# A third FFN with seven quarter products, and the modulation steps given out anew

## The chip, the cores and the metric

One Trainium2 chip, one core of it. The metric is device microseconds of one launch. The kernel before was timed three times: 2214.08, 2215.94 and 2216.86 us, median 2215.94 us.

## The reference, cut to what matters

Two layers over x of 512 tokens by 1024 features, all in float32. Each layer is FFN, mixer, FFN (the mixer is MLA attention in layer 0 and RWKV-7 in layer 1), and each of the six branches is modulated by vectors that come from one conditioning vector c:

```python
c_act = silu(c)
for i in range(2):
    mods = (c_act @ ada_w[i] + ada_b[i]).reshape(B, 3, 3, 1024)     # shift, scale, gate of three branches
    h = rmsnorm(x, g[i,0]) * (1 + mods[:,0,1]) + mods[:,0,0]
    x = x + 0.5 * mods[:,0,2] * swiglu(h, ffn_w_in[i,0], ffn_w_out[i,0])
    h = rmsnorm(x, g[i,1]) * (1 + mods[:,1,1]) + mods[:,1,0]
    x = x + mods[:,1,2] * mixer(h)                                  # MLA (i = 0), RWKV-7 (i = 1)
    h = rmsnorm(x, g[i,2]) * (1 + mods[:,2,1]) + mods[:,2,0]
    x = x + 0.5 * mods[:,2,2] * swiglu(h, ffn_w_in[i,1], ffn_w_out[i,1])
return rmsnorm(x, final_g)
```

`swiglu(h, w_in, w_out)` is `(silu(gate) * up) @ w_out` with `gate, up = split(h @ w_in)`; the inner width is 2816, that is 22 tiles of 128.

## The kernel before, in words

Activations lie transposed, 128 features by 512 tokens a tile, eight tiles for x and for h. Every float32 operand is split into a high and a low part in fp32r, and each product is three matmuls (high by high, high by low, low by high; `mm3`, lines 672 to 677). A weight tile of 128x1024 is loaded by SyncE's queue into one of three buffers (`wraw`, line 648), its high part is copied by ScalarE (`whigh`, line 662, four buffers each for high and low, `WB`), and its low part is subtracted by VectorE (`wlow`, line 668), after which the raw buffer is free again.

There are four FFNs, called (layer, place): (0,0), (0,1), (1,0), (1,1). (0,0) and (0,1) go through `ffn_plain` (line 879): in each of two halves of 11 inner tiles, the inner tiles are taken in pairs, each pair four weight tiles of eight products of 512 columns (96 matmuls), then eight output tiles `dn` of 33 matmuls each. The order of its instructions is the scheduler's. (1,0) and (1,1) go through `ffn` (line 928) with a `_Stream` (line 225): the first two pairs are plain (`pair_plain`), the other nine are computed by `pair_seven` (line 514), which multiplies 2x2 quarters with seven products in place of eight: 14 blocks of 12 matmuls of 256 columns. For this VectorE builds sums of the weights' quarters (`plan_pair`, line 347) and of h's (`plan_sums`, line 313). Here the order is written out by hand: all engines keep program order (`_InOrder`), and the preparing steps stand in one list with a cost each. After each piece of matmuls `beat` (line 426) adds `RATE` 0.72 per us of planned time to a credit, at most 2.0, and issues steps while the credit is positive, a weight buffer is free and the step's load was issued 4.0 planned us before. `need` issues what a product needs if it is not there yet. The pairs are in five parts (`PARTS`: pairs 0-1, 2-3, 4-5, 6-7, 8-10); after each of the first four, `down` (line 578) adds that part's share of the output, its first four tiles in two runs of inner tiles, the last part's share is the ordinary `down` (line 796) with its last tiles in halves of the tokens, so that the next norm can begin.

The modulation vectors: each of 128 steps (`mod_steps`, line 761) loads 512 KB of `ada_w` into a raw buffer of the same three and multiplies it on VectorE with `cact`, with the sum taken (line 768). 16 more are done at the start. The steps are one generator, in the order in which they are needed: the gate of (0,0) 8, then 16 and 8 for each of the other five branches. `pump(n)` draws the next n. In `ffn_plain` it draws 4 after each group of inner tiles (5 in FFN (0,1)), 1 after each output tile; in attention's out-projection, which is `down` too, 1 after each of five output tiles. So 58 steps stand in FFN (0,0), 5 in attention's out-projection and 65 in FFN (0,1); (1,0) and (1,1) have none.

In MLA, the value projections (`V`, lines 1102 to 1120) stand ahead of the attention loop; ScalarE's first Exp is that of the first head.

Of the kernel before, what the change touches and what calls it, by code (L numbers as in the profile page):

```python
# [35 lines left out]
SEVEN = (1, 0), (1, 1)  # L36
# [188 lines left out]
class _Stream:  # L225
# [19 lines left out]
    def plan(self):  # L245
        for f in (2, 3):
            for u in range(2):
                self.plan_tile(("plain", f, u), self.ffn_in[f, u].rearrange("p (k f) -> p k f", f=P), KT)
        self.norm.sums7 = [None] * (KT // 2)
        for i in range(KT // 2):  # L250
            self.plan_sums(i)
        for part in PARTS:
            for g in part:
                if g > 1:
                    self.plan_pair(g)
            if part is not PARTS[-1]:
                n = 2 * len(part)
                for m in range(0, KT, 2):
                    src = self.ffn_out[m:m + 2, :, 2 * part[0] * P:(2 * part[0] + n) * P].rearrange("m p f -> p m f")
                    self.plan_tile(("down", part[0], m), src, 2 * n)  # L260
        self.load()
# [34 lines left out]
    def plan_tile(self, name, src, n):  # L296
# [14 lines left out]
        self.add_split(high, low, after=((box, 0),))  # L311

# [113 lines left out]
    def beat(self, dt):  # L426
        self.now += dt
        self.credit = min(self.credit + RATE * dt, 2.0)
        while self.credit > 0 and self.can() and self.landed():
            self.step()  # L430
# [77 lines left out]
    def beats(self, dt):  # L508
        if self.outs:
            for f in self.outs.pop(0):  # L510
                f()
        self.beat(dt)
# [65 lines left out]
    def down(self, part0, n, g):  # L578
# [3 lines left out]
        for m0 in range(0, KT, 4):  # L582

            for run in (range(n // 2), range(n // 2, n)) if m0 == 0 else (range(n),):
                if run[-1] == n - 1 and m0 == 0:
                    self.flush()
                for m in range(m0, m0 + 4):
# [15 lines left out]
                    self.beats(0.68 * len(run))  # L603
# [5 lines left out]
class _Kernel:  # L609
# [151 lines left out]
    def mod_steps(self, l, s, part):  # L761
        nc = self.nc
        j0, j1 = (0, 16) if part == 0 else (16, 24)
        m = self.const.tile([P, j1 - j0], F32, name=f"mod_{l}_{s}_{part}")
        for j in range(j0, j1):
            raw = self.wraw(self.a["ada_w"][l, s * 24 + j].rearrange("p (k f) -> p k f", f=P), 8)
            raw2 = raw.rearrange("p k f -> p (k f)")
            nc.vector.scalar_tensor_tensor(raw2, raw2, 1.0, self.cact, op0=ALU.mult, op1=ALU.mult,  # L768
                                           accum_out=m[:, j - j0:j - j0 + 1])
            if j < j1 - 1:  # L770
                yield
        nc.vector.tensor_tensor(m, m, self.ada_b[:, l, s * 24 + j0:s * 24 + j1], op=ALU.add)
        if part == 0:
            A = self.const.tile([P, KT], F32, name=f"A_{l}_{s}")
            nc.vector.scalar_tensor_tensor(A, m[:, 8:16], 1.0, self.norm_g[:, l, s], op0=ALU.add, op1=ALU.mult)
            self.AB[l, s] = (A, m[:, 0:8])
        else:
            if s != 1:
                nc.vector.tensor_scalar(m, m, 0.5, None, op0=ALU.mult)
            self.gate[l, s] = m  # L780
        yield

    def pump(self, n=1):
        for _ in range(n):
            if next(self.mod_work, self) is self:
                break

    def mods_until(self, done, key):
        while key not in done:
            next(self.mod_work)  # L790
# [88 lines left out]
    def ffn_plain(self, l, j, norm, nxt):  # L879
# [3 lines left out]
        for half in range(2):  # L883
# [3 lines left out]
            while f0 < f_end:  # L887
# [25 lines left out]
                self.pump((5 if (l, j) == (0, 1) else 4) if f0 > 2 else 0)  # L913
# [6 lines left out]
            if half == 0:  # L920
                self.down(chunks, act, (l, s))
# [54 lines left out]
    def mla(self, norm, nxt):  # L976
# [123 lines left out]
        for _ in itertools.chain(kproj(0), kproj(1)):  # L1100
            pass
        V = {}
# [149 lines left out]
        self.down(self.out_chunks(a["mla_out"]), o, (0, 1), nx, (5, 6, 7), 1)  # L1252
# [662 lines left out]
    def setup(self):  # L1915
# [4 lines left out]
            self.mod_steps(l, s, p) for l in range(2) for s in range(3) for p in range(2) if (l, s, p) != (0, 0, 0))  # L1920
# [204 lines left out]
```

## Time and profile before

| | us |
|---|---|
| median of three runs | 2215.94 |
| the profiled execution | 2224.98 |
| its span, first to last instruction | 2223.2 |
| TensorE matmul busy | 2133.7 (96%) |
| VectorE busy | 1486.6 (67%) |
| ScalarE busy | 949.5 (43%) |
| mean granted TensorE clock | 0.985 of 2.4 GHz |

In the profile PE is TensorE's matmuls, PEld its weight loads, DVE VectorE, ACT ScalarE, POOL GpSimd, SP SyncE; a q behind a name is the engine's queue, which issues DMAs. Matmuls are pipelined: one matmul's own duration is longer than the distance between the starts of two, and the distance is what counts. L177 is the line of the helper through which all instructions of the hand-ordered stretches go, so there the tiles' names tell what is meant. An arrow in brackets behind a row names what ended the idle time before it.

### The profile page before, as it was taken

Reading aid. Unit: us, or ns where it says so; the run is one execution under the profiler, and the core shown is the slowest. Engines: PE = TensorE matmul, PEld = TensorE weight load, DVE = VectorE, ACT = ScalarE, POOL = GpSimd, SP = SyncE. Lnnn points to the kernel's source line nnn. Section 1 sums busy time; section 2 is a strip of 40 time slices with the busy share of each in tenths; the row PEclk is TensorE's granted clock in tenths of the full one; section 3 lists DMA queues with packets and bytes.
Section 4 is the critical chain, followed back from the end, with each engine's and each line's share of the span. In section 5 each row is a group of like instructions: output and inputs, shape, how many; then the busy total and the mean of one; then the engine's idle time right before and its main releaser. Section 6 shows DMA issues by size and latency. Waiting matters only on the chain.

```text
span 2223.2 us, 32341 instructions
## 1 busy us (share of the span) xinstructions
PE 2133.7 (96%) x12376; PEld 1862.1 (84%) x12376; DVE 1486.6 (67%) x2587; ACT 949.5 (43%) x1585; POOL 322.1 (14%) x362
## 2 busy tenths in 40 slices
PE   6999999999999999999999997999779999999998
PEld 5788888877798888888999997778678879899997
DVE  8755555678766655648777777845836666877785
ACT  3322323467533222234444455656535444444452
POOL 4100001023210000010000003514665001000001
PEclk9999999999999999999999998999989999999999
DMA  8765555201426665741322323236986532232322
GB/s 287 241 202 188 191 200 190 81 25 43 171 74 230 209 195 193 228 131 59 113 95 87 114 70 102 86 123 196 259 218 166 149 137 101 85 97 93 114 79 74
DMA packets 156555, 316.65 MB, mean 142 GB/s; under 512 B 55281, under 2 KB 73201, under 8 KB 156401
## 3 DMA queue, kind: packets, MB, share of 16 engines
q1 hardware_dynamic: 155104, 313.87, 43.7%
q8 instruction: 97, 1.59, 0.3%
q10 hardware_dynamic: 1296, 0.72, 0.1%
q14 instruction: 58, 0.47, 0.1%
HBM read 282.03 MB, written 32.51 MB: 141 GB/s over the span
## 4 chain that ended last, share of the span: by engine, by line
PE 80%; DVE 7%; DMA 5%; ACT 2%; POOL 2%; issue 2%; SPq 0%; DVEq 0%; ACTq 0%; POOLq 0%
PE up L177 18%; PE dn L177 8%; PE up L675 6%; PE up L677 6%; PE up L676 6%; PE dn L675 5%; PE dn L676 5%; PE dn L677 5%; PE pr L177 4%; PE q L177 2%; DMA wraw<-in_ada_w_dram 2%; PE a L177 2%; PE gram L177 1%; PE s L177 1%; PE ys L177 1%
## 5 line engine op out<-in xcount | busy, mean ns | idle before, releaser
L665 ACT ACTIVATE wh<-wraw 128x1024 fp32r<-128x1024 f32 (+4 forms) x185 | 170.1, 919 | 422.0 <-PE dn L676 142.8
L669 DVE TENSOR_TENSOR wl<-wraw,wh 128x1024 fp32r<-128x1024 f32 (+4 forms) x185 | 195.3, 1056 | 155.2 <-ACT wh L665 154.0
L675 PE MATMUL up<-h,wh 128*128 128x512 f32 (+1 forms) x776 | 286.7, 369 | 2.5 <-ACT silu L909 2.5
L676 PE MATMUL up<-h,wh 128*128 128x512 f32 (+1 forms) x776 | 287.1, 370 | 0.0
L677 PE MATMUL up<-h,wl 128*128 128x512 f32 (+1 forms) x776 | 286.7, 370 | 0.0
L74 POOL TENSOR_TENSOR sq<-sq,sq 128x512 f32<-128x512 f32 x27 | 37.5, 1389 | 1460.0 <-ACT sq L70 1446.2
L768 DVE SCALAR_TENSOR_TENSOR wraw<-wraw,cact 128x1024 f32<-128x1024 f32 x128 | 155.7, 1224 | 127.6 <-DMA wraw<-in_ada_w_dram 127.1
L177 DVE TENSOR_TENSOR wl<-wraw,wh 128x1024 fp32r<-128x1024 f32 (+2 forms) x129 | 151.6, 1176 | 99.4 <-ACT wh L177 99.1
L177 PE MATMUL up<-h,wh 128*128 128x256 f32 (+1 forms) x816 | 180.3, 316 | 2.9 <-DVE h L177 2.9
L177 ACT ACTIVATE wh<-wraw 128x1024 fp32r<-128x1024 f32 (+2 forms) x129 | 130.8, 1017 | 105.5 <-PE dn L177 53.5
L675 PEld LDWEIGHTS up<-h,wh 128*128 128x128 f32 x776 | 146.1, 188 | 27.3 <-ACT silu L909 2.9
L677 PEld LDWEIGHTS up<-h,wl 128*128 128x128 f32 x776 | 146.1, 188 | 24.7
L676 PEld LDWEIGHTS up<-h,wh 128*128 128x128 f32 x776 | 146.1, 188 | 24.6
L177 PE MATMUL up<-tsh,wh 128*128 128x256 f32 x576 | 163.0, 283 | 0.0
L177 PE MATMUL up<-tsl,wh 128*128 128x256 f32 x576 | 163.0, 283 | 0.0
L177 PE MATMUL up<-tsh,wl 128*128 128x256 f32 x576 | 163.0, 283 | 0.0
L177 PE MATMUL dn<-act,wh 128*128 128x512 f32 (+1 forms) x536 | 162.3, 385 | 0.0
L675 PE MATMUL dn<-act,wh 128*128 128x512 f32 x374 | 146.4, 391 | 2.5 <-ACT act L682 2.5
L177 PEld LDWEIGHTS up<-h,wh 128*128 128x128 f32 x816 | 136.1, 192 | 14.6 <-DVE h L177 4.2
L676 PE MATMUL dn<-act,wh 128*128 128x512 f32 x374 | 146.4, 391 | 0.0
L677 PE MATMUL dn<-act,wl 128*128 128x512 f32 x374 | 146.0, 390 | 0.0
L177 PE MATMUL up<-h,wl 128*128 128x256 f32 (+1 forms) x408 | 128.9, 316 | 0.0
(449 smaller groups left out, 5134.6 us busy)
## 6 DMA issues: line engine op xcount, KB each, us to landing
wraw<-in_ffn_in_dram SPq DMA_DIRECT2D x132, 512.0 KB, 4.0
wraw<-in_ada_w_dram SPq DMA_DIRECT2D x128, 512.0 KB, 4.0
wrawb<-in_ffn_in_dram SPq DMA_DIRECT2D x36, 512.0 KB, 4.0
wraw<-in_ffn_out_dram SPq DMA_DIRECT2D x32, 512.0 KB, 4.2
wraw<-in_ffn_out_dram SPq DMA_DIRECT2D x40, 384.0 KB, 3.5
wraw<-in_rwkv_rkv_dram SPq DMA_DIRECT2D x24, 512.0 KB, 3.2
wraw<-in_ffn_out_dram SPq DMA_DIRECT2D x32, 320.0 KB, 3.2
ada<-in_ada_w_dram SPq DMA_DIRECT2D x16, 512.0 KB, 4.2
```

What stands on the lines that cost most here:

```text
L74: nc.gpsimd.tensor_tensor(self.acc, self.acc, sq, op=ALU.add)
L177: self.tc.keep_in_program_order(op(*args, **kw))
L665: self.nc.scalar.activation(wh[:, :n], raw[:, :n], AF.Copy)
L669: self.nc.vector.tensor_tensor(wl[:, :n], raw[:, :n], wh[:, :n], op=ALU.subtract)
L675: mm(ps, wh, ah, start=first, stop=False)
L676: mm(ps, wh, al, start=False, stop=False)
L677: mm(ps, wl, ah, start=False, stop=last)
L768: nc.vector.scalar_tensor_tensor(raw2, raw2, 1.0, self.cact, op0=ALU.mult, op1=ALU.mult, accum_out=m[:, j - j0:j - j0 + 1])
```

## The change

`SEVEN` gets FFN (0,1), which goes through `_Stream` and `pair_seven` as (1,0) and (1,1) do. The modulation steps become pairs of a source and a function (`mod_part`), so that a stream can plan them: `plan_ada` puts 2 steps behind the first part's output tiles and 7 behind each of the next three, while steps are left. In `ffn_plain`, now FFN (0,0) alone, `pump` draws 6 after a group, 4 after the last but one and none after the last of a half, and 2 after each output tile of the first half (`down(..., pump=2)`); attention's out-projection draws 2 for 1. The steps then stand 72 in FFN (0,0), 10 in attention's out-projection, 23 in (0,1) and 23 in (1,0). The stream's credit may reach 3.5 for 2.0, and in the first run of `down` no step is issued but credit gathers. In MLA a one-element Exp on ScalarE is issued ahead of the value projections.

```diff
-SEVEN = (1, 0), (1, 1)
+SEVEN = (0, 1), (1, 0), (1, 1)
...
                     self.plan_tile(("down", part[0], m), src, 2 * n)
+                self.plan_ada(2 if part is PARTS[0] else 7)
...
+    def plan_ada(self, n):
+        for _ in range(n):
+            self.plan_mod()
+
+    def plan_mod(self):
+        step = next(self.k.mod_work, None)
+        if step is None:
+            return
+        box = {}
+        self.plan_load("raw", step[0], lambda t: t, box, 0)
+
+        def do():
+            step[1](box[0])
+            self.free("raw")
+        self.add(1.25, False, do, (box, 0))
...
-        self.credit = min(self.credit + RATE * dt, 2.0)
+        self.credit = min(self.credit + RATE * dt, 3.5)
...
-    def beats(self, dt):
+    def beats(self, dt, quiet=False):
         if self.outs:
             for f in self.outs.pop(0):
                 f()
-        self.beat(dt)
+        if quiet:
+            self.now += dt
+            self.credit += RATE * dt
+        else:
+            self.beat(dt)
...
-                    self.beats(0.68 * len(run))
+                    self.beats(0.68 * len(run), run[-1] < n - 1)
...
-    def mod_steps(self, l, s, part):
+    def mod_part(self, l, s, part):
...
         for j in range(j0, j1):
+            def do(raw, j=j):
+                raw2 = raw.rearrange("p k f -> p (k f)")
+                self.nc.vector.scalar_tensor_tensor(raw2, raw2, 1.0, self.cact, op0=ALU.mult, op1=ALU.mult,
+                                                    accum_out=m[:, j - j0:j - j0 + 1])
+                if j == j1 - 1:
+                    last()
+            yield self.a["ada_w"][l, s * 24 + j].rearrange("p (k f) -> p k f", f=P), do
...
-                self.pump((5 if (l, j) == (0, 1) else 4) if f0 > 2 else 0)
+                if f0 > 2 and f0 < f_end:
+                    self.pump((4, 6)[f0 < f_end - 1])
...
-                self.down(chunks, act, (l, s))
+                self.down(chunks, act, (l, s), pump=2)
...
+        warm = self.small("warm", [P, 1], bufs=1)
+        self.tc.keep_in_program_order(nc.scalar.activation(warm, self.ones, AF.Exp))
         V = {}
...
-        self.down(self.out_chunks(a["mla_out"]), o, (0, 1), nx, (5, 6, 7), 1)
+        self.down(self.out_chunks(a["mla_out"]), o, (0, 1), nx, (5, 6, 7), 2)
```

## Rows read from the trace of the kernel before

**Rows 1.** Busy us (share) xinstructions by engine, then the chain, by engine; from the page.

```profile
PE 2133.7 (96%) x12376; PEld 1862.1 (84%) x12376; DVE 1486.6 (67%) x2587; ACT 949.5 (43%) x1585; POOL 322.1 (14%) x362
...
PE 80%; DVE 7%; DMA 5%; ACT 2%; POOL 2%; issue 2%; SPq 0%; DVEq 0%; ACTq 0%; POOLq 0%
```

**Rows 2.** Busy time by stretch: start:end length, PE, PEld, DVE, ACT, POOL, clock, DMA share, GB/s.

```profile
636.21:1005.71 369.50, 366.76 (x1749) 308.38 (x1748) 214.01 (x343) 108.52 (x150) 7.96 (x7) 1.00 0.57 185
...
1005.71:1352.82 347.11, 346.98 (x2329) 321.55 (x2327) 255.19 (x380) 158.74 (x237) 8.54 (x7) 1.00 0.29 98
...
1862.16:2212.73 350.57, 350.45 (x2400) 326.48 (x2399) 258.23 (x399) 157.43 (x235) 8.50 (x10) 1.00 0.27 89
```

**Rows 3.** Timeline of TensorE, 944 to 949 us: start, us, what [idle before <-releaser].

```profile
947.64 0.77 PE L675 MATMUL dn<-act,wh 128*128 128x512 f32 x1 [2.49 <-ACT act L682]
```

**Rows 4.** Busy time by stretch: one plain pair; one part's two pairs; its output tiles.

```profile
840.70:862.47 21.77, 21.77 (x97) 18.02 (x96) 12.84 (x20) 6.50 (x9) 0.00 (x0) 1.00 0.63 217
...
1074.23:1114.54 40.31, 40.31 (x338) 40.31 (x337) 28.86 (x40) 22.59 (x34) 0.00 (x0) 1.00 0.36 118
...
1114.54:1136.33 21.79, 21.79 (x99) 18.02 (x98) 17.18 (x24) 5.74 (x8) 0.00 (x0) 1.00 0.21 73
```

**Rows 5.** Groups by line and form: busy us, mean ns | idle before.

```profile
L177 PEld LDWEIGHTS up<-tsh,wh 128*128 128x128 f32 x576 | 110.6, 192 | 0.0
...
L665 ACT ACTIVATE wh<-wraw 128x1024 fp32r<-128x1024 f32 x105 | 111.4, 1061 | 268.0 <-DMA wraw<-in_ffn_in_dram 114.5 <-PE up L676 53.7 <-PE dn L676 35.6
```

**Rows 6.** Timeline of ScalarE and TensorE around the first Exp.

```profile
454.41 1.28 ACT L1154 ACT_TABLE_LOAD   x1
...
455.71 0.69 ACT L1154 ACTIVATE p<-s,mx 128x512 f32<-128x512 f32 x1
...
460.32 0.38 PE L1143 MATMUL s<-k,qh 128*128 128x256 f32 x1 [0.88 <-ACT p L1154]
```

**Rows 7.** Timeline of SyncE's queue, VectorE and TensorE, 62 to 75 us.

```profile
62.53 4.16 SPq L651 DMA_DIRECT2D wraw<-in_ada_w_dram  x2
...
67.51 3.73 SPq L651 DMA_DIRECT2D wraw<-in_ffn_in_dram  x3
...
66.25 1.22 DVE L768 SCALAR_TENSOR_TENSOR wraw<-wraw,cact 128x1024 f32<-128x1024 f32 x1
...
67.40 1.22 DVE L768 SCALAR_TENSOR_TENSOR wraw<-wraw,cact 128x1024 f32<-128x1024 f32 x1
...
69.66 1.22 DVE L768 SCALAR_TENSOR_TENSOR wraw<-wraw,cact 128x1024 f32<-128x1024 f32 x1 [1.03 <-DMA wraw<-in_ada_w_dram]
...
72.92 1.23 DVE L669 TENSOR_TENSOR wl<-wraw,wh 128x1024 fp32r<-128x1024 f32 x1 [2.03 <-ACT wh L665]
...
74.86 0.50 PE L675 MATMUL up<-h,wh 128*128 128x512 f32 x1 [2.50 <-ACT silu L909]
```

**Rows 8.** Timeline of VectorE and TensorE, FFN (0,1): first weights of two pairs.

```profile
808.69 1.23 DVE L669 TENSOR_TENSOR wl<-wraw,wh 128x1024 fp32r<-128x1024 f32 x1 [3.43 <-ACT wh L665]
...
818.96 0.39 PE L677 MATMUL up<-h,wl 128*128 128x512 f32 x1
...
922.27 1.23 DVE L669 TENSOR_TENSOR wl<-wraw,wh 128x1024 fp32r<-128x1024 f32 x1 [2.05 <-ACT wh L665]
```

**Rows 9.** Timeline of VectorE and TensorE in attention's last quarter.

```profile
543.37 1.23 DVE L768 SCALAR_TENSOR_TENSOR wraw<-wraw,cact 128x1024 f32<-128x1024 f32 x1 [0.84 <-DMA wraw<-in_ada_w_dram]
...
545.05 0.50 PE L177 MATMUL o<-pt,v 128*128 128x256 f32 x2 [0.65 <-DVE pt L177]
```

**Rows 10.** Timeline of VectorE, FFN (1,0), from pair 3 to pair 4.

```profile
1121.41 0.75 DVE L177 SCALAR_TENSOR_TENSOR x<-dn,mod,x 128x512 f32<-128x512 f32 x1 [3.69 <-PE dn L177]
...
1124.80 1.22 DVE L177 TENSOR_TENSOR wl<-wraw,wh 128x1024 fp32r<-128x1024 f32 x1
...
1135.25 1.22 DVE L177 TENSOR_TENSOR wl<-ws,wh 128x1024 fp32r<-128x1024 f32 x1
```

**Rows 11.** DMA issues, from the page: KB each, us from issue to landing.

```profile
wraw<-in_ada_w_dram SPq DMA_DIRECT2D x128, 512.0 KB, 4.0
```

More of the change, by code (lines that the diff above doesn't have):

```diff
@@ L758, in rows, with last @@
         return rb[:, :n * P]
-    def mod_steps(self, l, s, part):
-        nc = self.nc
+    def mod_part(self, l, s, part):
         j0, j1 = (0, 16) if part == 0 else (16, 24)
         m = self.const.tile([P, j1 - j0], F32, name=f"mod_{l}_{s}_{part}")
-        for j in range(j0, j1):
[L766 to L781, printed above, removed]
+        def last():
+            nc = self.nc
+            nc.vector.tensor_tensor(m, m, self.ada_b[:, l, s * 24 + j0:s * 24 + j1], op=ALU.add)
+            if part == 0:
+                A = self.const.tile([P, KT], F32, name=f"A_{l}_{s}")
+                nc.vector.scalar_tensor_tensor(A, m[:, 8:16], 1.0, self.norm_g[:, l, s], op0=ALU.add, op1=ALU.mult)
+                self.AB[l, s] = (A, m[:, 0:8])
+            else:
+                if s != 1:
+                    nc.vector.tensor_scalar(m, m, 0.5, None, op0=ALU.mult)
+                self.gate[l, s] = m
+        for j in range(j0, j1):
+            def do(raw, j=j):
[5 more added lines that the diff above has]
+            yield self.a["ada_w"][l, s * 24 + j].rearrange("p (k f) -> p k f", f=P), do
@@ L783, in pump, with mod_step @@
+    def mod_step(self):
+        src, do = next(self.mod_work)
+        do(self.wraw(src, KT))
     def pump(self, n=1):
         for _ in range(n):
-            if next(self.mod_work, self) is self:
+            step = next(self.mod_work, None)
+            if step is None:
                 break
+            step[1](self.wraw(step[0], KT))
     def mods_until(self, done, key):
         while key not in done:
-            next(self.mod_work)
+            self.mod_step()
     def add_x(self, m, ps, g, sl=slice(0, S)):
@@ L1919, in setup @@
         self.mod_work = itertools.chain.from_iterable(
-            self.mod_steps(l, s, p) for l in range(2) for s in range(3) for p in range(2) if (l, s, p) != (0, 0, 0))
+            self.mod_part(l, s, p) for l in range(2) for s in range(3) for p in range(2) if (l, s, p) != (0, 0, 0))
         self.new_x()
```

## The prediction

> **What bounds the kernel now.** I read the page first: TensorE's matmuls are busy for 2133.7 of 2223.2 us and hold 80% of the chain that ended last; VectorE is at 67% [rows 1]. So an edit gains what it takes from TensorE's own row of matmuls, and it costs where VectorE, the three raw buffers or ScalarE come too late for the next matmul. Next, the stretches by stage [rows 2]. Measured from the last output matmul of one stage to that of the next, the plain FFN (0,1) takes 369.50 us with PE busy for 366.76. The two streamed FFNs take 347.11 and 350.57 with PE busy for all but 0.13 of it. VectorE is at 58% in (0,1), 74% in (1,0) and (1,1). The reader is to see two things: a streamed FFN leaves no hole in TensorE, and it has the fuller VectorE. In (0,1) there is one real hole, 2.49 us, and the matmul behind it lasts 0.77 us [rows 3] against a start every 0.227.
>
> **Part 1: FFN (0,1) by seven products.** A plain pair is 96 matmuls in 21.77 us, so 226.8 ns each; two quarter pairs are 336 matmuls in 40.31 us, so 120.0 ns each and 20.16 us a pair [rows 4]. Seven for eight would give an eighth; quarters of 256 columns cost 120.0 where half of 226.8 is 113.4, so 1.61 us a pair remain, and nine pairs give 14.5 us. The hole goes as well. The whole is better read from [rows 2]: after the change (0,1) has the structure of (1,1), parts, tail of four tiles and all, so its time is 350.57 in place of 369.50: **-18.9 us**. What (1,1) doesn't show is the norm behind a four-tile tail when it is of the "split" kind; I cost this at nothing, since the next FFN's first matmuls, on the first half of the tokens, cover the second half's norm.
>
> The Trainium skill (TensorE: Matmul & The Clock Gate, section Back-to-back issue gap) speaks against this part: it gives a sustained 131 ns per matmul of 512 columns and 81 ns at 128, set by weight load and matmul together. A straight line between the two, an estimate, puts 256 columns at 98 ns, a pair at 16.4 against 12.6 us, and the change would lose 35 us on nine pairs. The trace doesn't agree: 226.8 and 120.0 ns [rows 4].
>
> **Part 2: the early Exp.** ScalarE loads its table for 1.28 us right ahead of the first Exp, and TensorE then stands 0.88 us for that softmax [rows 6]. The load moves beside the value projections. **-0.9**; between 0 (TensorE waits for the chain of maxima anyway) and -1.3 (all of the load). By the Trainium skill (ScalarE: Activation LUTs, What ACT_TABLE_LOAD costs) a switch has a drain of 1.38 us on top, and the sum would be -13.9 by it. Here the Exp starts 0.02 us after the load, so no drain is seen behind it [rows 6].
>
> **Part 3: FFN (0,0) takes 72 steps for 58.** Steps share the three raw buffers with the weights, in order on SyncE's queue. At the start, four steps stand ahead of the next pair's weights. The first of these weights is loaded at 67.51, its low part is ready at 74.15, and TensorE restarts at 74.86 after 2.50 us of idleness [rows 7]. With six steps that load has to wait for the buffer of the fourth step, which VectorE leaves at 69.66 + 1.15 + 0.09 = 70.9: 3.4 us later. Then the low part is ready at 77.6; the low part is first read 0.45 us after the restart, so the restart is at 77.1: **+2.3**. Ends: 0, if the scheduler loads the weight first, and 5.7, if the SiLU that frees PSUM stays behind two weight copies and adds another 2.3 to the 3.4.
> Later pairs have ten loads for eight. In a free-running ring a step holds a buffer 4.0 [rows 11] + 1.15 us (distance of two steps, 66.25 to 67.40, [rows 7]), a weight 4.0 + 1.06 [rows 5] + 1.23: (6 x 5.15 + 4 x 6.3) / 3 = 18.7 us a pair, under 21.77. Against this stands FFN (0,1) with nine loads: its first weight tile was ready 9.0 us before use in the second half's first pair (808.69 + 1.23 against 818.96) and 4.3 us five pairs later (922.27 + 1.23 against 818.96 + 5 x 21.77 = 927.8) [rows 8], so there nine loads took 21.77 + 0.94 = 22.7 us. Ten would take 25.2. The first half has two more such pairs and no lead (2 x 3.46 = 6.9), the second four with a lead of 9.0 (4 x 3.46 - 9.0 = 4.8): up to 11.7 us. I take **0**, since what slows the ring in (0,1) are waits for TensorE to free a weight buffer, which go when the ring is late. The second step per output tile falls into a stretch with leads of this size and is within the same bounds.
>
> **Part 4: ten steps for five in attention's out-projection.** The scheduler draws these into attention's last quarter, where VectorE is the fuller engine. One step there, at 543.37, left TensorE idle for 0.65 us [rows 9]. Of five more, I take three there and two in the out-projection, whose VectorE has room: **+2.0**. Ends: 0 and 5 x 1.15 = 5.8.
>
> **Part 5: 23 steps in each of two streams.** A part lasts 62.1 us with VectorE busy for 28.86 + 17.18 = 46.0 [rows 4]; seven steps of 1.15 + 0.08 add 8.6: 88%. The step list puts them between a part's output weights and the next pair's sums, so these come later: the sum weights "wl<-ws" are ready at 1135.25 + 1.22 = 1136.5, and the pair that starts at 1136.33 reads them in its fifth block, 4 x 12 x 0.12 = 5.8 us later: 5.6 us of lead. VectorE idles 3.69 us at the beginning of the output tiles [rows 10], and three of the seven steps fit there, since VectorE takes them ahead of the first "x" of the run. Then 8.6 - 3.7 = 4.9 us remain against 5.6. With landings of 4.0 us between the steps that is about even; I take 0.5 us a boundary, three boundaries in two streams: **+3.0**. Ends: 0, and 5.0 each (below). The quiet run and the cap of 3.5 only set this order; in (1,1), which gets no steps, they cost nothing as TensorE has no hole there [rows 2].
>
> **Sum.** -18.9 - 0.9 + 2.3 + 2.0 + 3.0 = -12.5 us on an execution of 2224.98 (span 2223.2 and 1.8 around it): 2212.5. The median of the timed runs is 9.0 lower, 2215.94; the difference carried over gives **2203.4 us**. What a measurement tells from no change is 0.2%, 4.4 us.
>
> **Rivals.**
> *Nothing is paid.* The waits of parts 3 to 5 are all hidden: -19.8, 2196.1 us. For it: leads of 5 to 9 us [rows 8, 10]. Against it: the start, where the restart already hangs on the fourth step's buffer [rows 7].
> *FFN (0,0) becomes bound by the raw buffers.* The 11.7 us of part 3 in full: -0.8, 2215.1 us. For it: the falling lead in (0,1). Against it: that lead never reached zero in five pairs, and a free ring needs 18.7 us.
> *The streams fall behind, slower than before.* If the steps run only behind the quiet run, from 1114.54 + 21.79 / 4 = 1120.0 on, and in rounds of three buffers, 5.2 us each, then two rounds end at 1130.4; the third holds the seventh step and the next pair's weights, whose low part is ready 4.0 + 1.06 + 1.23 later, at 1136.7. From that low part, 1124.80 + 1.22, to the end of "wl<-ws" the trace has 10.4 us [rows 10], so the fifth block gets its weights at 1147.1 and not at 1136.3 + 5.8 = 1142.1: 5.0 us per boundary, 30 in six; -18.9 - 0.9 + 2.3 + 2.0 + 30.0 = +14.5, 2230.4 us. It decides from 15.5 / 6 = 2.6 us a boundary. Against it: VectorE's 3.69 us of idleness lie ahead of exactly this place.
> *Quarters are bound by their weight load.* PEld is busy for 40.31 of 40.31 us [rows 4], one load 192 ns [rows 5]. If each matmul had to wait for its own load, a pair would be 168 x 0.192 = 32.3 us and nine pairs 94 us longer: about 2310 us. The starts at 120.0 ns in two streams stand against it. The issue-gap rule of the Trainium skill, quoted above, is of this kind.
>
> **Chances.** Forecast, -8 to -17 us: 0.42. Nothing paid: 0.25. Raw buffers: 0.18, around no change. Streams behind: 0.11. Weight load: 0.02; the remaining 0.02 I give to no change. Faster by over 0.2%: nearly all of the first two and a third of the third, 0.73; within 0.2%: 0.13; slower: 0.14. The range leaves out most of the streams' case and the best tail of "nothing paid": 2195 to 2216 us; the likeliest case alone is 2199 to 2208.
>
> **What would show it.** (0,1), measured as in [rows 2], at 350 to 355 us; (1,0) at 347 to 351, with waits of "up" for "wl<-ws" at the start of pairs 4, 6 and 8, if part 5 is paid; the restart of (0,0) at about 77 us, and no waits of "up" or "dn" for "wl" behind it, if the ring holds; the table load ahead of the value projections and the 0.88 us gone. The prediction is wrong if (0,0) grows by over 8 us or a stream by over 8.

## The result, and the profile after

The changed kernel is slower. Its four runs took 2228.18 to 2238.01 us, median 2231.46, against 2215.17 (2214.08 to 2216.86) for the kernel before: ratio 1.0059 with a 95% interval of 1.0038 to 1.0080. Timed again with the experiments it took 2229.80 us (six runs) against 2218.07: 1.0050 (1.0032 to 1.0067). The prediction said 2203.4, with 2195 to 2216 as its range.

The page of the profile after, answering to [rows 1]: busy time by engine, then the chain by engine.

```profile
PE 2125.4 (95%) x13030; PEld 1883.8 (85%) x13030; DVE 1608.5 (72%) x2790; ACT 1002.2 (45%) x1678; POOL 324.7 (15%) x364
...
PE 72%; DVE 12%; DMA 8%; ACT 3%; issue 2%; POOL 2%; SPq 0%; DVEq 0%; ACTq 0%; POOLq 0%
```

TensorE's work has become less (2125.4 for 2133.7 us), but its share of the chain has fallen from 80 to 72%. VectorE and DMA have what it lost: TensorE now waits. The stretches by stage, as in [rows 2], say where. In order: FFN (0,0), attention, (0,1), (1,0), (1,1), columns as in [rows 2]. The fence behind it has the first two of these for the kernel before.

```profile
0.00:407.04 407.04, 377.14 (x1680) 311.56 (x1681) 262.22 (x403) 119.13 (x162) 39.15 (x25) 0.98 0.69 225
407.04:647.71 240.67, 236.75 (x1397) 197.37 (x1396) 184.76 (x412) 138.05 (x326) 58.23 (x72) 0.99 0.26 86
647.71:1007.97 360.26, 353.91 (x2403) 328.47 (x2402) 293.17 (x463) 162.20 (x242) 8.40 (x8) 1.00 0.43 136
1007.97:1359.35 351.38, 347.98 (x2329) 321.77 (x2327) 276.67 (x422) 159.11 (x238) 9.29 (x8) 1.00 0.39 125
1865.16:2215.69 350.53, 350.41 (x2400) 326.47 (x2399) 258.06 (x399) 157.43 (x235) 8.54 (x10) 1.00 0.29 89
```

```profile
0.00:394.74 394.74, 371.72 (x1680) 308.72 (x1681) 245.15 (x373) 119.78 (x162) 39.15 (x25) 1.00 0.64 213
394.74:636.21 241.47, 236.98 (x1396) 197.36 (x1396) 180.26 (x401) 138.67 (x326) 58.30 (x72) 0.99 0.23 77
```

(0,0) is 12.3 us longer, (0,1) only 9.2 shorter, (1,0) 4.3 longer; (1,1), which got no steps, is where it was.

**FFN (0,0): the weights' lead is used up.** In the middle output tiles the first low part of the second tile was ready at 156.21 + 0.95 us and first read at 165.28, 8.1 us ahead; six tiles on it is 205.54 + 0.96 and 210.16, 3.7 us ahead. Four loads per tile take 0.7 us more than the tile's 33 matmuls. (The rows at 151.62, 159.60 and 160.75 bear on the stall at 162.15, below.)

```profile
151.62 0.58 ACT L941 ACTIVATE silu<-up 128x512 f32<-128x512 f32 x1
...
156.21 0.95 DVE L691 TENSOR_TENSOR wl<-wraw,wh 128x768 fp32r<-128x768 f32 x1
...
159.60 1.23 DVE L803 SCALAR_TENSOR_TENSOR wraw<-wraw,cact 128x1024 f32<-128x1024 f32 x1 [2.43 <-DMA wraw<-in_ada_w_dram]
...
160.75 0.68 DVE L942 TENSOR_TENSOR silu<-silu,up 128x512 f32<-128x512 f32 x1
...
165.28 0.39 PE L699 MATMUL dn<-act,wl 128*128 128x512 f32 x1
...
205.54 0.96 DVE L691 TENSOR_TENSOR wl<-wraw,wh 128x768 fp32r<-128x768 f32 x1 [1.60 <-ACT wh L687]
...
210.16 0.39 PE L699 MATMUL dn<-act,wl 128*128 128x512 f32 x1
```

Then come the pairs with six steps. TensorE's restart, and the stalls in the output tiles, in a late pair and in the tail (start, us, what, idle before and its releaser):

```profile
75.94 0.56 PE L697 MATMUL up<-h,wh 128*128 128x512 f32 x1 [4.07 <-ACT wh L687]
...
162.15 0.49 PE L697 MATMUL dn<-act,wh 128*128 128x512 f32 x1 [1.01 <-ACT act L704]
...
304.28 0.50 PE L697 MATMUL up<-h,wh 128*128 128x512 f32 x1 [0.80 <-ACT wh L687]
...
389.82 0.38 PE L697 MATMUL dn<-act,twh 128*128 128x256 f32 x1 [2.95 <-ACT twh L704]
```

Adding up by how much each matmul starts later than its regular distance behind the one before (226.7, 120 and 113 ns by size), and taking off the same sum of the kernel before, gives 3.5 us at the start, 1.8 in the middle output tiles, 2.4 in the second half's pairs and 5.1 in the tail. The stall at 162.15 is not one of late weights: ScalarE had the SiLU ready at 151.62 + 0.58 = 152.20, and its product on VectorE ran at 160.75, behind two steps, the second of which had waited 2.43 us for its data. VectorE in one of the pairs, with ScalarE's copy for the third weight, shows the mechanism for the weights:

```profile
257.21 1.23 DVE L691 TENSOR_TENSOR wl<-wraw,wh 128x1024 fp32r<-128x1024 f32 x1 [2.48 <-ACT wh L687]
...
261.86 1.06 ACT L687 ACTIVATE wh<-wraw 128x1024 fp32r<-128x1024 f32 x1 [0.70 <-DMA wraw<-in_ffn_in_dram]
...
264.06 1.23 DVE L803 SCALAR_TENSOR_TENSOR wraw<-wraw,cact 128x1024 f32<-128x1024 f32 x1 [3.00 <-DMA wraw<-in_ada_w_dram]
...
265.21 1.22 DVE L691 TENSOR_TENSOR wl<-wraw,wh 128x1024 fp32r<-128x1024 f32 x1
268.60 1.22 DVE L803 SCALAR_TENSOR_TENSOR wraw<-wraw,cact 128x1024 f32<-128x1024 f32 x1 [2.17 <-DMA wraw<-in_ada_w_dram]
...
275.36 1.23 DVE L803 SCALAR_TENSOR_TENSOR wraw<-wraw,cact 128x1024 f32<-128x1024 f32 x1 [0.90 <-DMA wraw<-in_ada_w_dram]
...
278.00 1.23 DVE L803 SCALAR_TENSOR_TENSOR wraw<-wraw,cact 128x1024 f32<-128x1024 f32 x1 [1.41 <-DMA wraw<-in_ada_w_dram]
...
280.58 1.22 DVE L691 TENSOR_TENSOR wl<-wraw,wh 128x1024 fp32r<-128x1024 f32 x1 [0.94 <-ACT wh L687]
```

VectorE stands 3.00 + 2.17 + 0.90 + 1.41 = 7.5 us in front of steps whose data is still under way. The weight's low part at 265.21 starts without a gap behind such a step: its high part was there at 261.86 + 1.06 = 262.92, so it stood 2.3 us behind that step, and its buffer came free later, and the next load with it. From this pair's first "wl" to the next pair's VectorE needs 280.58 - 257.21 = 23.4 us, where TensorE needs 21.77. Not every pair is slower than TensorE: measured so, the six with six steps take 22.7 and 20.1 us in the first half and 21.9, 21.5, 23.4 and 23.7 in the second, 22.2 in the mean. The Trainium skill (PSUM — Partial Sum Buffer, section Engine vs sequencer instructions) calls VectorE's queue strictly first in, first out; the trace agrees (265.21).

**Streams: seven steps at a boundary.** SyncE's queue, VectorE, ScalarE and TensorE between the first and second part of (0,1):

```profile
768.01 0.33 SPq L289 DMA_DIRECT2D wraw<-in_ada_w_dram  x1
769.74 4.06 SPq L289 DMA_DIRECT2D wraw<-in_ffn_in_dram  x3
...
772.22 1.21 DVE L177 SCALAR_TENSOR_TENSOR wraw<-wraw,cact 128x1024 f32<-128x1024 f32 x1
...
774.58 1.22 DVE L177 TENSOR_TENSOR wl<-wraw,wh 128x1024 fp32r<-128x1024 f32 x1 [1.14 <-ACT wh L177]
776.96 1.23 DVE L177 TENSOR_TENSOR wl<-wraw,wh 128x1024 fp32r<-128x1024 f32 x1 [1.15 <-ACT wh L177]
...
783.47 1.06 ACT L177 ACTIVATE wh<-ws 128x1024 fp32r<-128x1024 f32 x1 [2.13 <-DVE ws L177]
784.44 0.58 ACT L177 ACTIVATE c<-up 128x512 f32<-128x512 f32 x1
...
785.14 2.35 DVE L177 TENSOR_TENSOR wl<-ws,wh 128x1024 fp32r<-128x1024 f32 x2
...
785.07 0.39 PE L177 MATMUL up<-tsh,wh 128*128 128x256 f32 x1 [1.02 <-ACT c L177]
...
786.40 0.58 PE L177 MATMUL up<-tsh,wl 128*128 128x256 f32 x1 [0.84 <-DVE wl L177]
```

The pair's weights get a buffer only when the fifth step leaves one (769.74); VectorE is through the seventh step at 772.22 + 1.21 = 773.4, and "wl<-ws" comes at 785.14 + 1.2, where the pair's fifth block wanted it about 2 us earlier. The first wait names ScalarE's copy "c": its input, the pair's first product, had been there since about 781 (two blocks of 12 matmuls at 0.12 us from the pair's start at 778.13), but it stood behind "wh<-ws" in ScalarE's queue, and that on VectorE's sums. So both waits are one. The same pair of waits stands at all five boundaries with seven steps; by the sum of late starts they cost 3.8, 2.3, 2.0, 2.2 and 2.2 us. At the sixth, with three steps, there is none. In the second profile of the kernel after the five cost 3.8, 2.4, 3.8, 4.4 and 2.6.

### The profile page after: what moved, and what is told of

It is laid out like the page before. It is cut to its first block, busy times and chain, and to the rows that moved or that the text cites. A ratio compares the mean times of both kernels' runs of the same rounds, so it can differ in the third digit from the quotient of the medians.

```text
span 2226.4 us, 33900 instructions
## 1 busy us (share of the span) xinstructions
PE 2125.4 (95%) x13030; PEld 1883.8 (85%) x13030; DVE 1608.5 (72%) x2790; ACT 1002.2 (45%) x1678; POOL 324.7 (15%) x364
## 4 chain that ended last, share of the span: by engine, by line
PE 72%; DVE 12%; DMA 8%; ACT 3%; issue 2%; POOL 2%; SPq 0%; DVEq 0%; ACTq 0%; POOLq 0%
PE up L177 26%; PE dn L177 9%; PE pr L177 4%; PE dn L697 4%; PE dn L698 4%; PE dn L699 4%; DMA wraw<-in_ada_w_dram 3%; DMA wraw<-in_ffn_in_dram 3%; PE q L177 2%; PE a L177 2%; PE up L699 2%; PE up L698 2%; PE up L697 2%; DVE wl L177 1%; PE s L177 1%
## 5 line engine op out<-in xcount | busy, mean ns | idle before, releaser
L177 PEld LDWEIGHTS up<-h,wh 128*128 128x128 f32 x1168 | 193.3, 191 | 17.7 <-DVE h L177 4.3
L687 ACT ACTIVATE wh<-wraw 128x1024 fp32r<-128x1024 f32 (+3 forms) x120 | 107.5, 897 | 192.3 <-DMA wraw<-in_ffn_in_dram 90.7
L691 DVE TENSOR_TENSOR wl<-wraw,wh 128x1024 fp32r<-128x1024 f32 (+3 forms) x120 | 124.8, 1042 | 77.7 <-ACT wh L687 77.1
L177 PEld LDWEIGHTS dn<-act,wh 128*128 128x128 f32 x792 | 147.4, 188 | 29.4
L177 PEld LDWEIGHTS up<-tsh,wh 128*128 128x128 f32 x864 | 166.2, 192 | 5.3 <-ACT c L177 5.3
L177 PEld LDWEIGHTS up<-tsh,wl 128*128 128x128 f32 x864 | 166.2, 192 | 5.2 <-DVE wl L177 5.2
L697 PE MATMUL up<-h,wh 128*128 128x512 f32 (+1 forms) x456 | 162.9, 357 | 4.9 <-ACT wh L687 4.9
L177 PEld LDWEIGHTS up<-tsl,wh 128*128 128x128 f32 x864 | 166.2, 192 | 0.0
L699 PE MATMUL up<-h,wl 128*128 128x512 f32 (+1 forms) x456 | 163.3, 358 | 0.9 <-DVE wl L691 0.8
L698 PE MATMUL up<-h,wh 128*128 128x512 f32 (+1 forms) x456 | 163.1, 358 | 0.0
L177 PE MATMUL dn<-act,wl 128*128 128x512 f32 (+1 forms) x396 | 153.1, 387 | 0.0
```

The costliest lines, as they stand in the source:

```text
L177: self.tc.keep_in_program_order(op(*args, **kw))
L687: self.nc.scalar.activation(wh[:, :n], raw[:, :n], AF.Copy)
L691: self.nc.vector.tensor_tensor(wl[:, :n], raw[:, :n], wh[:, :n], op=ALU.subtract)
L697: mm(ps, wh, ah, start=first, stop=False)
L698: mm(ps, wh, al, start=False, stop=False)
L699: mm(ps, wl, ah, start=False, stop=last)
```

## The experiments

The stages of all profiled executions, in us (cut as in [rows 2]; the time mix is what lies between (1,0) and (1,1)), then profiled execution, median and ratio to the kernel before with its interval. Two things are to be known for reading it. The cut behind (1,0) lies ahead of the next norm's first sums, and the stage's very last output matmul ends 2.0 us later in every kernel; the expectations from "load only" on give (1,0) up to that last matmul, so their 349 is 347 here. And in "product only", "own buffers" and the three "moved" the scheduler drew all steps of attention's out-projection forward into (0,0), which there has 82 or 83 of them.

| kernel | (0,0) | attention | (0,1) | (1,0) | time mix | (1,1) | profiled | median | ratio |
|---|---|---|---|---|---|---|---|---|---|
| before | 394.74 | 241.47 | 369.50 | 347.11 | 509.34 | 350.57 | 2224.98 | 2215.94 | |
| before, again | 398.05 | 239.02 | 365.46 | 347.09 | 507.35 | 350.58 | 2220.32 | 2219.24 | 0.9996 (0.9987-1.0004) |
| after | 407.04 | 240.67 | 360.26 | 351.38 | 505.81 | 350.53 | 2228.18 | 2231.46 | 1.0059 (1.0038-1.0080) |
| after, again | 405.68 | 239.05 | 361.79 | 354.07 | 505.25 | 350.55 | 2228.62 | 2229.80 | 1.0050 (1.0032-1.0067) |
| no stream steps | 409.26 | 239.08 | 351.54 | 347.01 | 506.74 | 350.52 | 2217.48 | 2217.01 | 0.9988 (0.9976-0.9999) |
| (0,0) as before | 396.32 | 239.61 | 362.04 | 351.08 | 508.09 | 350.52 | 2220.12 | 2218.57 | 0.9998 (0.9985-1.0011) |
| neither | 397.06 | 238.15 | 351.59 | 346.98 | 506.78 | 350.58 | 2203.96 | 2205.46 | 0.9937 (0.9923-0.9951) |
| load only | 394.30 | 237.14 | 358.43 | 349.28 | 504.93 | 350.56 | 2207.93 | one run | |
| product only | 397.09 | 236.81 | 355.76 | 348.05 | 506.04 | 350.54 | 2206.52 | one run | |
| own buffers | 401.03 | 237.66 | 360.05 | 354.45 | 504.81 | 350.57 | 2220.86 | 2218.20 | 0.9996 (0.9986-1.0006) |
| four a boundary | 408.61 | 241.21 | 351.84 | 351.26 | 506.65 | 350.57 | 2222.54 | 2221.22 | 1.0011 (1.0002-1.0020) |
| moved, 1 | 401.38 | 237.98 | 353.09 | 347.02 | 515.23 | 350.53 | 2217.47 | 2216.26 | 0.9989 (0.9978-1.0001) |
| moved, 2 | 402.52 | 236.59 | 352.64 | 347.03 | 510.02 | 350.53 | 2212.06 | 2211.36 | 0.9959 (0.9946-0.9973) |
| moved, 3 | 403.99 | 237.97 | 352.23 | 347.04 | 509.54 | 350.52 | 2214.03 | 2213.34 | 0.9960 (0.9946-0.9973) |

**Before, again** (nothing edited).

> The kernel before, run and profiled once more. Its profiled execution took 2224.98 us, 9 us above the median of its timed ones, while the profiled execution of the kernel after (2228.18) was the shortest of its four: the two profiles differ by 3.2 us, the medians by 16. If the profile of before was a slow draw, the new profiled execution takes 2214 to 2218 us, and the rows by stage show which stage was 9 us longer in the old one. If profiling itself costs this kernel 9 us, the new profile shows 2224 to 2226 again with every stage as before.

The new profile took 2220.32 us, near the median of 2219.24, so profiling does not cost 9 us, and the first profile lay above the usual time; but it is not as low as the 2214 to 2218 expected. The median had moved too: 2218 to 2220 us in all later rounds, for the 2215.94 of the first three runs. The difference of 4.7 us is spread: (0,1) 4.0 shorter, attention 2.4, the time mix 2.0, (0,0) 3.3 longer. In (0,1) the hole of [rows 3] is simply not there, TensorE is busy for all but 0.33 us:

```profile
637.07:1002.53 365.46, 365.13 (x1749) 307.38 (x1748) 213.81 (x343) 108.65 (x150) 7.96 (x7) 1.00 0.59 187
```

**No stream steps**, **(0,0) as before**, **neither**: the two suspects taken out singly and together.

```diff
+        if self.k.leave:          # a stream's steps: taken, neither loaded nor multiplied
+            step[1](None)
+            return
```

> Kernel after without the 46 steps of the two streamed FFNs (0,1) and (1,0): their loads and products are left out, the other 82 stay. Theory A (the steps delay the weight sums at five boundaries): FFN (0,1) takes 350 to 351 us for 360.3, FFN (1,0) 347 for 351.4, no stall at the third product of pairs 4, 6 and 8; about 14 us faster than the kernel after, 2215 to 2218, with FFN (0,0) as long as in the kernel after. Rival B (the quarters themselves are dearer in (0,1), or TensorE loses its clock there): (0,1) stays near 360 and the time within 5 us of the kernel after.

```diff
-                if f0 > 2 and f0 < f_end:
-                    self.pump((4, 6)[f0 < f_end - 1])
+                self.pump(4 if f0 > 2 else 0)
...
-                self.down(chunks, act, (l, s), pump=2)
+                self.down(chunks, act, (l, s))
...
-        self.down(self.out_chunks(a["mla_out"]), o, (0, 1), nx, (5, 6, 7), 2)
+        self.down(self.out_chunks(a["mla_out"]), o, (0, 1), nx, (5, 6, 7), 1)
```

> Kernel after with FFN (0,0) and attention's out-projection as in the kernel before: 58 and 5 steps where after has 72 and 10; the 19 steps in between are left out, the streams keep their 46. Theory A (ten loads for eight per pair and four for three per output tile use up the lead of the weights): the last output matmul of (0,0) ends at 394 to 396 us for 407.0, with no stall in the output tiles of its first half nor in its last pairs; 10 to 13 us faster than after. Rival B (something else in the kernel after makes (0,0) longer, such as the order that the scheduler gives its instructions): over 400 us. The streams keep their stalls in both.

> Both of these together: 63 steps as in the kernel before, the other 65 left out, FFN (0,1) by seven products and the early Exp. Theory A: what is left is the gain of the seven products, so 18 to 20 us faster than the kernel before, 2195 to 2198, and the two single effects add up. Rival B: at most 8 us faster than before.

Theory A holds, and nearly in size: without the streams' steps (0,1) and (1,0) take 351.54 and 347.01 us, and (0,0) stays long; with (0,0) as before it ends at 396.32, and the streams keep their stalls. In timed ratios the first is worth 0.6%, the second 0.5%, both together 1.13% (1.0050 to 0.9937). What remains in "neither", the seven products and the early Exp, is 0.63% (0.49 to 0.77) faster than before: 14 us, not the 18 to 20 that were expected; the early Exp was not run by itself. The stage says why: (0,1) at 351.59 is 13.9 us under the 365.46 of the second profile, and 17.9 under the first.

**Load only** and **product only**: each step cut into its halves.

```diff
+                c = slice(0, P)
-                self.nc.vector.scalar_tensor_tensor(raw2, raw2, 1.0, self.cact, ...
+                self.nc.vector.scalar_tensor_tensor(raw2[:, c], raw2[:, c], 1.0, self.cact[:, c], ...
```

> Kernel after with every step's 512 KB load and its buffer as it is, but the product over the first 128 of 1024 columns only (the other 896 are left out), so VectorE's share of a step falls from 1.23 to about 0.2 us. Theory A1 (FFN (0,0) is held up by landings: ten loads in three raw buffers, and a VectorE that stands in order before a step whose data is still under way): (0,0) ends within 5 us of the kernel after, 402 to 409 us. Rival A2 (VectorE's time for the products): it ends at 394 to 398. In the streams, theory V (8.6 us of VectorE ahead of the weight sums): the stalls at the third product go, (0,1) 351 to 353 us, (1,0) 349 to 350. Rival R (the pair's weights wait for the steps' buffers): the stalls stay at 1.5 us or more each, (0,1) over 356.

```diff
-        self.plan_load("raw", step[0], lambda t: t, box, 0)
...
+        self.add(1.25, False, lambda: step[1](None))
...
-                self.nc.vector.scalar_tensor_tensor(raw2, raw2, 1.0, self.cact, op0=ALU.mult, op1=ALU.mult,
+                self.nc.vector.scalar_tensor_tensor(self.cact, self.cact, 0.0, self.cact, op0=ALU.mult, op1=ALU.add,
```

> The counterpart: every step is an instruction of VectorE of 1024 columns on the vector that lies in SBUF, without a load and without a raw buffer (the modulation's weights are left out). Theory A1: FFN (0,0) ends at 394 to 398 us, as with no added steps; rival A2: 402 to 409. In the streams, theory V: stalls of 1.5 us or more at the five boundaries stay, (0,1) 356 to 361; rival R: they go, 351 to 353.

Both are single executions. In (0,0) neither half costs anything alone (394.30 and 397.09 us), though DMA moves 232 GB/s with the loads alone. So A1 and A2 are both wrong as stated: it is the round of a buffer, landing and product one behind the other, with the weights' low parts in the same queue, that is too long; cut either and it fits. In the streams the halves differ. With loads alone the stalls stay at all five boundaries (1.8, 2.8, 0.9, 1.3 and 1.0 us, 7.9 in all for 12.5 in the kernel after), and (0,1) keeps 6.9 of its 8.7 us, (1,0) 2.3 of 4.4; VectorE waits for most of the steps there and never works for long. With products alone one boundary of five stalls, for 1.0 us. So the loads and their buffers weigh more, as rival R says, but three of the five stalls are under the 1.5 us that it named, and the products are not free: alone they leave 0.9 to 1.4 us of the lead of 5.7 at four boundaries, as the prediction's 4.9 us of VectorE would. It takes both for the full stall. VectorE's steps with loads alone at the first boundary, which now need 0.3 us each:

```profile
751.22 0.29 DVE L177 SCALAR_TENSOR_TENSOR wraw<-wraw,cact 128x128 f32<-128x128 f32 x1 [0.67 <-DMA wraw<-in_ada_w_dram]
...
752.47 0.29 DVE L177 SCALAR_TENSOR_TENSOR wraw<-wraw,cact 128x128 f32<-128x128 f32 x1 [0.95 <-DMA wraw<-in_ada_w_dram]
...
753.74 0.29 DVE L177 SCALAR_TENSOR_TENSOR wraw<-wraw,cact 128x128 f32<-128x128 f32 x1 [0.97 <-DMA wraw<-in_ada_w_dram]
```

With products alone (0,1) is still 4.2 us longer than without steps: 1.0 us is that one stall, some 1.5 are smaller delays of 0.3 to 0.4 us, and the rest is its tail, where TensorE waits 1.05 us for GpSimd's squares (0.72 without steps) and its clock then falls (granted 0.72 in the mean from 978 to 984 us).

**Own buffers** for the steps of (0,0) and of attention's out-projection.

```diff
-            step[1](self.wraw(step[0], KT))
+            step[1](self.adaw(step[0]))       # 128x1024 of pool "k", three buffers, idle here
```

> Kernel after, complete, with the steps of FFN (0,0) and of attention's out-projection loaded into three buffers of their own (those of the streams' second raw pool, idle until then) in place of the weights' three raw buffers. Theory A1: a pair's four weight loads have their buffers to themselves, (0,0) ends at 394 to 399 us for 407 to 409, and the kernel is 8 to 12 us faster than after, about as fast as before (2216 to 2222 where before takes 2215 to 2220). Rival A3 (the DMA rate, not the buffers: 220 to 237 GB/s in this stage): (0,0) stays over 404.

0.5% faster than after, as expected in size, so DMA's rate is not the limit (A3 falls: 241 GB/s in this stage, and it is shorter). But (0,0) is at 401.0, for 394 to 399: the stalls for weights are gone, and one hole of 4.8 us has appeared at 155 us, where SiLU's product stands on VectorE behind steps that the scheduler now places earlier (40 steps have run by then, for 26 in the kernel after). The product itself is no later than in the kernel after: there too it ran 8.5 us after its input was ready, here 8.2. There TensorE came to it 5.8 us later, and lost 1.0 us.

**Four a boundary.**

```diff
-                self.plan_ada(2 if part is PARTS[0] else 7)
+                self.plan_ada(2 if part is PARTS[0] else 4)
...
-        self.down(self.out_chunks(a["rwkv_out"]), o, (1, 1), nx, (5, 6, 7), tags="CBA")
+        self.down(self.out_chunks(a["rwkv_out"]), o, (1, 1), nx, (5, 6, 7), 2, tags="CBA")
```

> Kernel after, complete, with four steps for seven between a part's output weights and the next pair's sums in both streams; the seven that are left over go to the out-projection behind the second time mix, two per output tile. The boundary with three steps in (1,0) showed no stall and those with seven 2.0 to 3.5 us, so four should leave 0 to 0.5: (0,1) 351 to 353 us for 360.3, (1,0) 349 to 350 for 353.3, and 10 to 13 us less than after in all, if the out-projection hides its second step. If a boundary's stall comes from the quiet run and not from the steps, they stay near 2 us.

All five stalls are gone, (0,1) is at 351.84; so the quiet run is not their cause. (1,0) missed (351.26 in the table, 353.2 to its last matmul, for 349 to 350): the seven steps that fell into its last output tiles leave TensorE idle once, for 2.25 us, ahead of the norm's sums. 0.39% faster than after, a little less than expected.

**Moved, 1 to 3, and after again**: complete kernels, each from what the one before showed.

```diff
+                self.pump((4 * half, 6)[f0 < f_end - 1])          # 1: own buffers, four a boundary,
+        self.down(self.out_chunks(a["mla_out"]), ..., 3)          #    none in (1,0)'s last tiles
+                self.plan_ada(2 if part is PARTS[0] else 5)       # 2: five a boundary, the middle
+                self.own = False                                  #    output tiles' steps in "wraw"
+                self.pump((4 * half, 4 + 2 * half)[f0 < f_end - 1])   # 3: four per group, first half
```

> Complete kernel with the seven products in three FFNs and the steps placed by the runs so far: (0,0) and attention's out-projection use the three idle buffers, 68 steps in (0,0) with none behind the last group of its first half (there the run with own buffers had a hole of 4.9 us, since SiLU's product stood behind five steps on VectorE), three per output tile in attention's out-projection, four at a boundary of the streams, none in the output tiles of (1,0), where seven had cost 2.4 us and more, the last 13 around the second time mix's out-projection. Worked out by stage: (0,0) 394 to 397, attention 238, (0,1) 352, (1,0) 349, time mix 505, (1,1) 350.6: about 2200 to 2203 us, 0.6 to 0.9% faster than before and 1.2 to 1.4% than after. Rival: VectorE's order makes a new hole wherever steps are bunched (three per tile in the out-projection, five in a lump ahead of the time mix's), and it comes out within 4 us of before.

> The kernel after once more, on the same chip as the kernel before in the same rounds. From the runs with parts left out (2217.0 without the streams' steps, 13.8 us of stage time; 2218.6 with (0,0) as before, 12.0 us) it should take 2230 to 2231 us, 0.5 to 0.6% over before. If the first four runs (2228 to 2238) were a slow draw, it takes 2222 to 2226.

> The complete kernel with moved steps, mended in two places that the run before showed: the steps of the output tiles in the middle of (0,0) go back to the weights' three buffers (with buffers of their own five of them had been put ahead of SiLU's product on VectorE, and TensorE stood 6.6 us), and the streams get five steps per boundary for four, so that seven and not 13 are left for the time mix's out-projection (8 us longer with 13). If both holes came from that: (0,0) 394 to 398 us for 401.4, time mix 505 for 513.3; the streams show what five steps at a boundary cost, (0,1) 352 to 354, (1,0) 349 to 350; the kernel takes 2200 to 2206, 0.5 to 0.8% less than before. Rival: the scheduler puts steps ahead of SiLU's product whichever buffers they use, (0,0) stays at 400 or more, and the kernel within 0.3% of before.

> One more step from the run before: the hole of 6.1 us at the beginning of the first half's output tiles stayed, behind a SiLU product that stood on VectorE behind six steps per group. Here the first half's groups take four steps for six (as in the kernel before), the six go to attention's out-projection (four per output tile for three) and to the time mix's. If the steps ahead of SiLU's product are the cause, the hole shrinks below 1.5 us, (0,0) takes 395 to 398 us for 402.5 and the kernel 2203 to 2207, 0.5 to 0.75% less than before. Rival: the hole comes from the weights of the output tiles, whose low parts stand behind the same steps, or from the buffers of their own as such: it stays over 4 us and the time within 2 us of the run before.

The kernel after, again, came out where the runs with parts left out had put it (2229.80 us). The first of the moved ones missed, and its rival came true (2216.26 us, within 4 of before): its streams came out about as forecast (353.09, 347.02), but its hole in (0,0) grew to 6.6 us and 13 steps around the time mix's out-projection cost 8. The second mends some 5 of the latter 8 (510.02 for 515.23) and beats both kernels: 0.41% faster than before (0.27 to 0.54), 0.9% faster than after. It missed its 2200 to 2206 us as well, since (0,0) stayed at 402.52. Its streams (0,1) and (1,0) show that five steps at a boundary cost nothing there: no start is late at any of the six boundaries, and (0,1)'s 1.1 us over the kernel without steps come mainly from a wait where its last part's output tiles begin. At the first boundary the first sum weight is ready at 772.45 + 1.22 and read at 775.51, 1.8 us ahead:

```profile
639.11:991.75 352.64, 351.16 (x2402) 326.77 (x2402) 286.80 (x451) 162.52 (x242) 8.30 (x8) 1.00 0.41 130
991.75:1338.78 347.03, 346.95 (x2328) 321.56 (x2327) 275.10 (x416) 158.90 (x238) 9.29 (x8) 1.00 0.39 123
...
772.45 1.22 DVE L177 TENSOR_TENSOR wl<-ws,wh 128x1024 fp32r<-128x1024 f32 x1
...
775.51 0.28 PE L177 MATMUL up<-tsh,wl 128*128 128x256 f32 x1
```

The hole in (0,0) stayed in the second (6.07 us) and in the third (5.72 us, 2213.34 us in all, for under 1.5 and 2203 to 2207), where fewer steps were meant to end it. VectorE and TensorE of the third:

```profile
159.91 1.23 DVE L803 SCALAR_TENSOR_TENSOR adaw<-adaw,cact 128x1024 f32<-128x1024 f32 x1 [2.00 <-DMA adaw<-in_ada_w_dram]
...
161.26 1.23 DVE L803 SCALAR_TENSOR_TENSOR adaw<-adaw,cact 128x1024 f32<-128x1024 f32 x1
...
162.41 0.68 DVE L952 TENSOR_TENSOR silu<-silu,up 128x512 f32<-128x512 f32 x1
...
163.81 0.80 PE L697 MATMUL dn<-act,wh 128*128 128x512 f32 x1 [5.72 <-ACT act L704]
```

SiLU's product still follows steps that wait for their data. But the third was no test of the count: with fewer steps per group the scheduler drew others forward, and by the hole 42 steps had run, for 41 in the second. Its rival (the buffers of their own as such) stayed possible too, since only the kernels with such buffers have 40 steps or more by then. How to keep the hole out was not settled; with it gone the second kernel would be some 6 us faster, an estimate from its 6.07 us of idleness.

## Why the prediction was wrong, point by point

- **Part 1 (-18.9)** was mis-sized, not mistaken. Its core holds: quarters at 120 ns in a third FFN, and nine pairs' 14.5 us are what the runs show (13.9 against the second profile of before). The other 4.0 were the hole of [rows 3] and the slow matmuls behind it, which belonged to one execution. I then counted them a second time: that execution lay 9.0 us above its median, and I took the gain from the execution and the offset from the median. (Some 2 to 4 of the 9.0 were the median's: later rounds put it at 2218 to 2220.) The split norm behind the four-tile tail, which I had put at nothing, goes with about 1 us (351.6 for 350.57).
- **Part 2 (-0.9)** did not come. The table load is at 460.82, ahead of the value projections, and TensorE still stands 0.88 us in the same place, now with no load ahead; the low end of my bounds, 0, was right, and so was its reason. The Exp that TensorE waits for starts when VectorE's maximum is there, and it did so before the change too: at 459.60, 3.9 us behind the table load of [rows 6]. I had tied the wait to a load that had nothing to do with it.

```profile
460.82 1.28 ACT L1136 ACT_TABLE_LOAD   x1
...
471.86 0.58 ACT L1189 ACTIVATE p<-s,mx 128x384 f32<-128x384 f32 x1 [0.24 <-DVE mx L1183]
...
472.58 0.39 PE L1178 MATMUL s<-k,qh 128*128 128x256 f32 x1 [0.88 <-ACT p L1189]
```

- **Part 3, start (+2.3)**: right in kind. The restart is 1.1 us later (75.94 for 74.86) and the next matmuls run at half the clock (granted 0.53 from 76.0 to 79.6 us); 3.5 us in all.
- **Part 3, later pairs and output tiles (0, "up to 11.7")** is the first step that failed, by about 9 us. I set a free ring of 18.7 us a pair against the 25.2 worked out from (0,1)'s nine loads, and explained the latter away by waits for TensorE. The trace after shows 22.2 in the mean, and 23.4 and 23.7 in the two pairs after which TensorE stalls. The ring was not free: in-order VectorE waits for each step's data and holds the weights behind it. The second step per output tile, which I dismissed in one sentence, alone took 4.4 us of lead, and the tail, which I had not looked at, lost 5.1 us. The row with the falling lead had been the better guide, but that its 11.7 comes near the 9.3 lost is in part luck: 6.9 of it were to fall in the first half's pairs, where nothing was late, and 4.8 in the second's, which lost 2.4. My own sign of being wrong, (0,0) longer by over 8 us, is the one that came.
- **Part 4 (+2.0)**: attention with ten steps took 240.67, 239.05, 239.08 and 241.21 us, with five (and the early Exp) 239.61 and 238.15: +1.1 in the mean, less than what one execution differs from the next (2.4 us between the two of before). Where the scheduler had drawn all ten away it took 236.6 to 238.0.
- **Part 5 (+0.5 a boundary)** is the second step that failed: 2.0 to 3.8 at five boundaries. (They are five and not six, since four of (1,0)'s steps were taken in (0,1)'s last output tiles.) I had the lead right, and charged VectorE's busy time, 4.9 us of 5.6, with the landings set to "about even". The charge was right for the products alone; what failed is that the landings in shared buffers came on top. Measured, the first sum weights come 5.7 us ahead with no steps, 1.8 to 3.0 with five, and about 2 us late with seven: the last two cost 2 to 2.5 us each, where I had 1.23. A round of three buffers, (4.6 us of landing, the median of the seven at the boundary shown, + 1.2 of product) / 3 = 1.9, is near it. The rival "streams fall behind" had this round and the right place; its price of 5.0 was too high by some 2.8 in (1,0), since VectorE had the first weights' low part ready at 1135.07 + 1.23, which is 1134.1 on the clock of the trace before, and not at 1136.7.
- **The sum.** With the measured terms (seven products and Exp -14, (0,0) and out-projection +11.5, streams +14) the kernel is some 11 us slower than before; 11 to 13 were timed. The rivals that priced the raw buffers and the streams came true in part, in different stages, and the chances had treated them as alternatives. That the second one's 2230.4 us is close to the time measured is luck: it had 30 us in the streams, none behind the start in (0,0), and a gain of 19.8 from the first two parts.

## What to carry to other kernels

Steps that share a few landing buffers with the critical loads are to be priced by the buffer's whole round (landing, plus the wait in an in-order queue, plus the product, over the number of buffers), not by their engine time; as long as some lead is left they are free (three to five steps a boundary here), and beyond it each costs about its round. Where the trace has a nearby stretch with one load fewer, and its lead is falling already, a reason to expect no loss from one load more needs a row of its own; the pace worked out from it was too slow here (25.2 us a pair for 22.2 measured), and the free ring's too fast (18.7). An estimate made against one profiled execution must not count that execution's bad luck as gain: hold its stages against a second profile first.

## What the runs showed of the hardware

TensorE's clock fell behind some holes and not behind others. Granted clock (the sixth number behind the length, counts in brackets aside) of three stretches of the kernel after:

```profile
851.20:856.20 5.00, 4.17 (x35) 3.97 (x34) 5.00 (x7) 3.59 (x6) 0.00 (x0) 1.00 0.26 79
786.40:789.60 3.20, 3.19 (x15) 3.20 (x16) 3.20 (x5) 1.96 (x3) 0.00 (x0) 0.50 0.16 28
390.00:397.00 7.00, 6.06 (x29) 5.85 (x30) 4.50 (x6) 3.22 (x6) 1.87 (x2) 0.52 0.77 257
```

Ahead of the second TensorE had stood 1.02 and 0.84 us, ahead of the third 2.95 and 0.94, and it then ran at 1.2 GHz for 3.2 and 7 us: 256-column matmuls every 213 ns for 120, some 1.4 and 2.7 us on top of the holes (15 and 29 matmuls by 0.093). Ahead of the first it had stood 0.97 and 0.83 us, nearly as long as ahead of the second, and kept 2.4 GHz. So like stalls cost 2.3 and 3.8 us at two boundaries of one run. In the second profile of the same kernel it fell behind three of the five boundaries, and not always behind the longer waits: at the first after 1.00 and 0.83 us, at the fifth not after 1.26 and 0.84. The stretches behind these two:

```profile
783.40:786.80 3.40, 3.40 (x18) 3.40 (x19) 3.40 (x5) 1.97 (x3) 0.00 (x0) 0.60 0.16 45
...
1211.94:1215.34 3.40, 3.40 (x28) 3.40 (x29) 3.40 (x5) 2.44 (x4) 0.00 (x0) 1.00 0.19 41
```

What decides it these rows do not show. With three falls for one, and somewhat longer waits, the five boundaries cost 17.0 us in the second profile and 12.5 in the first.
